# Attention on one core: a planner's order replaced by a written table, with 15 instead of 16 groups of scores on VectorE

## The chip, the cores and the metric

The kernel runs on one core of a Trainium2 chip. The metric is the device time of one execution in microseconds (us). Five engines run side by side, each through its own list of instructions in order, and wait for each other by semaphores: TensorE (PE, with its weight loads as PEld), VectorE (DVE), ScalarE (ACT), GpSimd (POOL) and SyncE (SP), which only issues DMAs here.

## The reference, cut to what matters

Softmax attention over 8 x 8 heads, 512 positions, 64 numbers each, in 32-bit floats:

```python
scores = np.einsum('bhqd,bhkd->bhqk', q, k) / np.sqrt(64)
scores = scores - scores.max(axis=-1, keepdims=True)
attn = np.exp(scores)
attn = attn / attn.sum(axis=-1, keepdims=True)
out = np.einsum('bhqk,bhkd->bhqd', attn, v)
```

## The kernel before, in words

**Tiling.** The 64 heads are worked on as 32 pairs, numbered g = 0 to 31. A head has four blocks of 128 keys. The scores of one block are a tile of 128 keys x 512 queries, and two blocks make a *group*: `[128, 2, 512]` in PSUM, tile `st`, of which there are three buffers. There are 128 groups' worth of scores; the last group is done in two halves (numbers 127 and 128). The maximum is not subtracted.

**The way of one pair.**
- SP loads q, k and v of a pair, 256 KB each (`load`, L509). Each of the three has seven buffers, so a load waits until the buffer of seven pairs earlier has been cast.
- POOL casts each to 16 bits (`cast`: q and k at L525, v at L515). For v a column of ones stands beside the 64 columns, so that the last product also gives the sum of the exponentials.
- PE transposes q and k (`transposes`, L558, four matmuls a call, two calls a pair), and DVE copies the result to SBUF (`copy`, L571).
- PE makes the scores of a group (`scores`, two matmuls at L598 on 64 rows each).
- The exponential of most groups is one ACT instruction over 128x1024 numbers (L602). For some groups DVE makes it in place of ACT: a `raise` (L625) that reads the scores and leaves integer bits in `pd`, and five passes in SBUF (`pass`, number 0 to 4: L642, L651, L659, L661, L665), which leave two factors, `pe` and `pd`. Such a block needs two products where the others need one.
- PE multiplies with v (`values`, L704), one call for 128 queries of one head: four matmuls, and one more for each of its blocks that DVE has made. Seven such units share a PSUM bank `o`.
- For each bank DVE takes the reciprocal of the sums (`rec`, L671) and multiplies (`mul`, L676) into `ring`, which has 112 slots. SP stores from there (`store`, L690 for a pair of heads, L694 for one; the last two go through ACT's queue).
- The last head is done apart (`last`, L720; `finish`, L733 to L740).

**What sets the order.** All instructions are recorded in one order by hand, and each engine keeps its share of it. In the kernel before, the class `Plan` makes this order: it steps through a modelled time with costs for each operation (for instance `EXP` 853 and `EXP_FIXED` 64 ns) and writes down what each engine would do next. The 16 groups in `ON_DVE` go to DVE. `Plan.trigger` chooses behind which VectorE instruction a cast is held: `cast_behind` (L539 and the lines after it) adds a wait of the cast on one of the last six VectorE instructions. Casts before 9000 ns of the planned time have no such wait. For q and k a one-element `memset` on POOL (tile `mark`, L543) waits for the transposes that read the old buffer. In `scores`, the exps of the groups in `KNOWN` also wait for the cast six places back.

The first pair, groups 0 to 2, is written out in `first_pair`; the plan begins with group 3.

Of the kernel before, what the change touches and what calls it, by code (L numbers as in the profile page):

```python
# [17 lines left out]
class Plan:  # L18

    SLOT, EXP, EXP_DONE, EXP_FIXED = 216, 853, 181, 64  # L20
    INTO, OUT_OF = 96, 96
    TRANSPOSE, V_UNIT = 222, 128
    TO_ACT, TO_DVE, TO_PE = 220, 210, 60

    COPY, NORM, RAISE = (601, 690), (50, 133), (1132, 1215)
    RECIPROCAL = 115
    SCALE, PRODUCT, EXTRA = 333, 600, 29
    COPY_1 = (400, 190)
    NORM_COLUMN, PASS_DONE = 67, 115
    PASSES = (SCALE, SCALE, PRODUCT, SCALE, PRODUCT)  # L30
    BITS = 2
    NEEDS = (None, None, 0, 2, 3)
    FIRST_EXP = 5000
    STEP = 5
    CALM, KEEN = 9000, 4
    FIRST_UNIT = 4
    KNOWN, OVER = (13, 15, 18, 20, 22, 24, 27, 42, 50, 61, 69, 97), 6
    ON_DVE = (5, 10, 16, 25, 28, 39, 44, 54, 63, 66, 74, 81, 91, 96, 103, 116)

    LATE_NORM, LATE_COPY, HURRY, SOON, BACKLOG = 700, 1500, 800, 160, 600  # L40
    LATE_MUL, WAIT = 400, 200
    SLACK, AHEAD = 0, 2

    CAST, CAST_PORT, CAST_DONE, TO_POOL = 557, 475, 130, 150
    SCALE_PORT, PRODUCT_PORT, GAP, REACH = 271, 537, 20, 5
    FIRST_LAND, LOAD, STORE, LATENCY, ISSUE = 5200, 752, 376, 2300, 470
    QUEUED, URGENT = 3500, 16
    PAIRED, STORE_ISSUE = 18, 520
    RAW, QK16, NV, NU = 7, 5, 12, 112
    PAIR, DUEK, DUEV, DUEL, PRE = 3300, 3550, 6000, 5000, 0  # L50

    def __init__(self, groups, pairs, first):
        self.groups, self.pairs = groups, pairs
        self.pe, self.act, self.dve = 7000, self.FIRST_EXP, 6300
        self.pool, self.port, self.dma = 4600, 4600, self.FIRST_LAND
        self.m, self.tiled = first, True
        self.read = []
        self.exps = {}
        for m in range(first):
            self.act += self.EXP + self.EXP_FIXED  # L60
            self.exps[m] = self.act + self.EXP_DONE
            self.read.append(self.exps[m])
        self.tq = {0: 5800}
        self.transposed = {0: 5800}
        self.next_t = 1
        self.part_t = 0
        self.banks = [5100, 5800]
        self.todo = [(g, h) for g in range(pairs) for h in range(2)]
        self.last = self.todo.pop()
        self.last_part = 0  # L70
        self.head = None
        self.units = self.FIRST_UNIT
        self.member = {b: m for m, grp in enumerate(groups) for b in grp}
        self.ready = []
        self.passes = []
        self.passed = {}
        self.raised = set()
        self.steps = []
        self.busy_dve = 0
        self.order, self.paired = [], 0  # L80

        late = {grp[0][0] for m, grp in enumerate(groups) if m in self.ON_DVE}
        due = []
        for g in range(pairs):
            scores = 5000 + self.PAIR * g
            if g:
                due += [(scores - self.DUEK, g, "k"), (scores - self.DUEK + 10, g, "q")]
            due.append((scores + self.DUEV + (self.DUEL if g in late else 0), g, "v"))
        self.due = sorted(due)
        self.uncast = list(self.due)  # L90
        self.casts = []
        self.landed, self.cast_done = {}, {}
        self.first_loads = [(g, n) for _, g, n in self.due if g < self.RAW]
        self.first_loads += [(self.RAW, "k"), (self.RAW, "q")]
        for x in self.first_loads:
            self.dma += self.LOAD
            self.landed[x] = self.dma
        self.loads, self.stores, self.stored = [], [], []
        self.sp = 1650 + 470 * len(self.first_loads)

    def note(self, t, *what):
        self.steps.append((t, len(self.steps)) + what)

    def trigger(self, t):

        ops = self.ops
        if not ops or ops[-1][1] <= t - 300:  # L110
            return 1, None
        n = len(ops) - 1
        while (
            n > 0
            and len(ops) - n < self.REACH
            and not ops[n][2]
            and ops[n][0] - ops[n - 1][1] <= self.GAP
        ):
            n -= 1
        if n > 0 and ops[n][0] - ops[n - 1][1] <= self.GAP:  # L120
            n -= 1
        return len(ops) - n, ops[n][1]

    def emit(self, t, back, after):
        _, g, n = self.uncast.pop(0)
        shared = (g, n) == (1, "q")
        self.note(t, "cast", g, n, back if t > self.CALM else 0)
        if not shared:
            self.casts.append((g, n, t if after is None else after + self.TO_POOL))
        if g + self.RAW < self.pairs:  # L130
            self.loads.append((g + self.RAW, n))

    def fits(self, t, soon=0):
        if not self.uncast:
            return False
        _, g, n = self.uncast[0]
        if n != "v" and g >= self.QK16 and self.transposed.get(g - self.QK16, 1e9) > t:
            return False
        return self.landed.get((g, n), 1e9) <= t + soon

    def step_pool(self, t):
        if self.uncast and self.uncast[0][1:] != (1, "q") and not self.casts and self.pool <= t:
            quiet = not self.passes and self.port <= t and not any(x[1] == "raise" for x in self.ready)
            if self.fits(t) and (quiet or self.uncast[0][0] - self.PRE < t):
                self.emit(t, 1, None)
        if self.casts and self.pool <= t and self.port <= t:
            g, n, after = self.casts[0]
            if after <= t and self.landed.get((g, n), 1e9) <= t:
                self.casts.pop(0)
                begin = max(self.pool, self.port, after, self.landed[(g, n)])  # L150
                self.pool = begin + self.CAST
                self.port = begin + self.CAST_PORT
                self.cast_done[(g, n)] = begin + self.CAST + self.CAST_DONE

    def step_sp(self, t):
        if self.sp > t or (self.loads and self.dma > t + self.QUEUED):
            return
        urgent = len(self.stores) > self.URGENT
        if self.loads and not urgent:
            g, n = self.loads[0]  # L160
            if self.cast_done.get((g - self.RAW, n), 1e9) <= t:
                self.loads.pop(0)
                self.note(t, "load", g, n)
                self.dma = max(self.dma, t + self.LATENCY - self.LOAD) + self.LOAD
                self.landed[(g, n)] = self.dma
                self.sp = t + self.ISSUE
                return
        if self.stores and self.stores[0] <= t:
            both = self.both()
            if both and (len(self.stores) < 2 or self.stores[1] > t):  # L170
                return
            heads = 2 if both else 1
            self.note(t, "store", heads)
            self.dma = max(self.dma, t + self.LATENCY - heads * self.STORE) + heads * self.STORE
            for _ in range(heads):
                self.stores.pop(0)
                self.stored.append(self.dma)
            self.paired += heads - 1
            self.sp = t + self.STORE_ISSUE

    def both(self):

        n = len(self.stored)
        g, h, u = self.order[n]
        return (
            self.paired < self.PAIRED
            and g < self.pairs - 2
            and h == 0
            and n + 1 < len(self.order)
            and self.order[n + 1][0] == g  # L190
            and u % self.NU + 8 <= self.NU
        )

    def room(self, t, u):
        heads = (u - self.NU - self.FIRST_UNIT + 3) // 4
        return heads <= 0 or len(self.stored) >= heads and self.stored[heads - 1] <= t

    def free(self, n=0):
        m = self.m + n
        if m >= len(self.groups):  # L200
            return 1e9
        g = self.groups[m][0][0]
        return max(0 if m < 3 else self.read[m - 3], self.tq.get(g, 1e9))

    def for_dve(self, m):
        return m in self.ON_DVE
# [692 lines left out]
```

## Time and profile before

| | |
|---|---|
| time, median of 3 runs | 113.64 us (113.58 to 113.94) |
| the profiled execution | 113.92 us, of which 112.1 us are the span from its first instruction to its last |
| granted TensorE clock | 0.994 of full speed |
| moved by DMA | 33.84 MB, 302 GB/s on average, 336 to 382 GB/s from 11 to 81 us |
| scores on ACT at full width (L602) | 108 of 128x1024, and 2 of half that |
| groups on DVE (L625) | 16 |

The profile page gives the busy time of each engine, a chain of waits that ended last, and groups of instructions by line. An exp that is recorded as started while the one before it still runs looks longer than it is, so several exps can overlap in the sums. Queries of the trace show instructions in order of time, waits by who ended them, and busy time by window. The span of 112.1 us is counted from the first instruction of the program; the profiled execution's own time has 1.8 us more around it.

### The profile page before, as it was taken

What the parts mean: (1) busy time and instruction counts of PE and PEld (TensorE: products, weight loads), DVE (VectorE), ACT (ScalarE), POOL (GpSimd) and SP (SyncE); (2) the same over time, 40 slices, a digit from 0 to 9 for tenths busy, and PEclk for the clock granted to TensorE, in tenths of its full rate; (3) what the DMA queues carried; (4) which work ended last, traced back from release to release, by engine and by line L of the source; (5) the groups of instructions that cost most, each with busy time, mean ns of one, the idle gap of its engine ahead of it and who ended that gap; (6) DMA issues with size and microseconds to landing.
All of it is one profiled execution on the core that took longest, in us unless ns stands there. A gap on an engine that the chain in (4) does not pass through costs nothing.

```text
span 112.1 us, 4408 instructions
## 1 busy us (share of the span) xinstructions
PE 103.2 (92%) x1728; PEld 69.4 (62%) x1728; DVE 100.8 (90%) x227; ACT 105.5 (94%) x118; POOL 65.9 (59%) x127
## 2 busy tenths in 40 slices
PE   7978889999799998999989999899999999999980
PEld 7634555766367766658647767577557577675660
DVE  1647999999999999999999999999999999997390
ACT  4599999999999999999999999999999999999970
POOL 2147768549756886495594786876784855600000
PEclk9999999999999999999999999999999999999997
DMA  3999999999999999999999999999999974142354
GB/s 106 276 359 353 345 350 347 355 336 349 345 347 336 341 346 343 354 364 375 370 358 382 350 355 377 354 372 362 343 366 305 349 245 143 52 141 99 97 167 161
DMA packets 35093, 33.84 MB, mean 302 GB/s; under 512 B 2304, under 2 KB 35072, under 8 KB 35072
## 3 DMA queue, kind: packets, MB, share of 16 engines
q1 hardware_dynamic: 34496, 33.04, 90.4%
q10 hardware_dynamic: 576, 0.52, 1.4%
q8 instruction: 13, 0.21, 0.8%
q14 instruction: 8, 0.07, 0.2%
HBM read 25.17 MB, written 8.39 MB: 299 GB/s over the span
## 4 chain that ended last, share of the span: by engine, by line
DVE 39%; PE 24%; DMA 15%; issue 8%; POOL 7%; SPq 3%; ACT 2%; POOLq 0%; ACTq 0%
PE o L704 13%; DMA v<-in_v_dram 10%; PE st L598 8%; DVE pd L625 8%; DVE tqk L571 7%; DVE ring L676 7%; DMA q<-in_q_dram 5%; DVE m L659 4%; POOL qkp L525 4%; DVE pd L665 4%; POOL vp L515 3%; PE tp L558 2%; SPq L509 2%; DVE m L642 2%; DVE pe L651 2%
## 5 line engine op out<-in xcount | busy, mean ns | idle before, releaser
L602 ACT ACTIVATE pt<-st 128x1024 f16<-128x1024 f32 (+1 forms) x110 | 100.3, 1144 | 0.2 <-PE st L598 0.2
L704 PEld LDWEIGHTS <-pt 128*128 128x128 f16 x880 | 38.8, 98 | 12.1 <-issue 10.2
L704 PE MATMUL o<-vp,pt 128*128 128x65 f16 x880 | 45.3, 194 | 0.4 <-POOL vp L515 0.2
L598 PE MATMUL st<-tqk 64*128 64x512 f16 (+1 forms) x250 | 41.7, 380 | 2.6 <-ACT pt L602 1.4
L525 POOL CAST qkp<-k 128x512 f16<-128x512 f32 x31 | 22.2, 717 | 11.3 <-DVE rc L671 5.3
L525 POOL CAST qkp<-q 128x512 f16<-128x512 f32 x30 | 21.7, 725 | 9.0 <-DVE rc L671 5.3
L515 POOL CAST vp<-v 128x512 f16<-128x512 f32 x32 | 21.4, 679 | 9.2 <-PE st L598 2.4
L676 DVE TENSOR_TENSOR ring<-o,rc 128x448 f32<-128x448 f32 (+2 forms) x37 | 22.3, 606 | 0.4
L704 PE MATMUL o<-vp,pe 128*128 128x65 f16 x128 | 21.8, 194 | 0.0
L704 PE MATMUL o<-vp,pd 128*128 128x65 f16 x128 | 21.7, 192 | 0.0
L558 PE MATMUL tp<-ident,qkp 128*128 128x128 f16 x248 | 19.6, 220 | 1.6 <-DVE tqk L571 0.8
L558 PEld LDWEIGHTS <-qkp 128*128 128x128 f16 x248 | 14.4, 97 | 9.9 <-issue 4.6
L571 DVE COPY tqk<-tp 128x1024 f16<-128x1024 f16 x30 | 20.3, 683 | 0.0
L625 DVE TENSOR_SCALAR pd<-st 128x1024 uint16<-128x1024 f32 x16 | 19.5, 1216 | 0.7 <-PE st L598 0.7
L598 PEld LDWEIGHTS <-tqk 64*128 64x128 f16 x250 | 10.7, 93 | 11.8 <-issue 4.6
L704 PEld LDWEIGHTS <-pe 128*128 128x128 f16 x128 | 12.5, 98 | 3.4 <-issue 3.3
L704 PEld LDWEIGHTS <-pd 128*128 128x128 f16 x128 | 12.5, 98 | 0.0
L659 DVE TENSOR_TENSOR m<-m 128x1024 f16<-128x1024 f16 x16 | 11.0, 685 | 0.0
L665 DVE TENSOR_TENSOR pd<-pd,m 128x1024 f16<-128x1024 f16 x16 | 10.9, 684 | 0.0
L671 DVE RECIPROCAL rc<-o 128x7 f32<-128x7 f32 (+2 forms) x37 | 7.4, 199 | 2.6 <-PE o L704 2.4
L661 DVE TENSOR_SCALAR m<-m 128x1024 f16<-128x1024 f16 x16 | 6.7, 418 | 0.1
L651 DVE TENSOR_SCALAR pe<-pd 128x1024 uint16<-128x1024 uint16 x16 | 6.6, 411 | 0.0
(51 smaller groups left out, 34.9 us busy)
## 6 DMA issues: line engine op xcount, KB each, us to landing
v<-in_v_dram SPq DMA_DIRECT2D x32, 256.0 KB, 5.8
k<-in_k_dram SPq DMA_DIRECT2D x31, 256.0 KB, 5.8
q<-in_q_dram SPq DMA_DIRECT2D x31, 256.0 KB, 5.9
out_dram<-ring SPq DMA_DIRECT2D x18, 256.0 KB, 5.5
out_dram<-ring SPq DMA_DIRECT2D x25, 128.0 KB, 2.2
k<-in_k_dram ACTq DMA_DIRECT2D x2, 128.0 KB, 2.8
q<-in_q_dram SPq DMA_DIRECT2D x2, 128.0 KB, 2.6
out_dram<-ring ACTq DMA_DIRECT2D x2, 128.0 KB, 1.9
```

The source lines that it names most:

```text
L515: return nc.gpsimd.tensor_copy(out=vps[g % NV][:, :, :, 0:D], in_=raw[g]["v"][:, :, :, :])
L525: return nc.gpsimd.tensor_copy(out=dst, in_=src[:, :, :, :])
L558: reads[g] = nc.tensor.transpose(tps[g][:, n, i, :], qkp[g][:, n, i, :], ident)
L571: nc.vector.tensor_copy(out=tqk[g][:, :, :], in_=tps.pop(g).rearrange("p n i c -> p n (i c)"))
L598: nc.tensor.matmul(st[:, x, cols], kc, qc[:, cols], start=True, stop=True)
L602: ins = nc.scalar.activation(out=pt[:, :, cols], in_=st[:, :, cols], func=EXP, scale=scale, bias=SHIFT)
L625: nc.vector.tensor_scalar(out=r["pd"][:, :, :], in0=r["st"][:, :, :], scalar1=BITS, scalar2=BIAS, op0=AluOp.mult, op1=AluOp.add,)
L651: ins = nc.vector.tensor_scalar(out=r["pe"][:, :, :], in0=u[:, :, :], scalar1=0x7C00, scalar2=None, op0=AluOp.bitwise_and,)
L659: ins = nc.vector.tensor_tensor(out=m16, in0=m16, in1=m16, op=AluOp.mult)
L665: ins = nc.vector.tensor_tensor(out=u16, in0=u16, in1=m16, op=AluOp.mult)
L676: nc.vector.tensor_tensor(out=ring[:, u % NU : u % NU + n, :], in0=o[:, x : x + n, 0:D], in1=rcs.pop(u)[:, 0:n].broadcast_to([P, n, D]), o ...
L704: nc.tensor.matmul(os[u // 7][:, u % 7, :], part[:, y * P : (y + 1) * P], vps[g % NV][:, h, c, :], start=(n == 0), stop=(n == len(parts) - 1),
```

## The change

The class `Plan` is gone. A class `Order` holds the order as text instead: one letter for each step (`S` scores, `T` transposes, `V` values of one unit, `C` copy, `R` raise, the letters of `LETTERS` the passes, `N` reciprocal, `M` normalise, `K` cast, `G` load, `w` and `W` stores of one head and of two, `L` and `F` the last head), and beside it the order of heads, casts, loads and banks. A third number in `CASTS` says behind which VectorE instruction a cast is held, counted back from the last one recorded: 2 to 5 for all casts but the first seven, which have none (most often 2). In the order before these numbers run from 1 to 6.

- 15 groups are on DVE where there were 16; the last of them is group 108, where it was 116. The group taken off it is an ACT instruction more, a raise and five passes less, and eight matmuls less at `values`.
- Scores, transposes, values, copies, casts, loads and stores keep their number, apart from that; their places change. Steps of scores that follow each other without other TensorE work between make 91 runs, where they made 74.
- The first 21 loads are the same, but in another order from the 13th on. Of the 73 loads behind them the order changes throughout: the first is pair 9's q, and pair 8's k and q come fifth and sixth.
- `raise_` takes its tiles `pe` and `pd` when it is recorded, where `scores` took them earlier.
- `KNOWN` and the number of buffers of every pool stay as they were; `first_pair` is not changed.

```diff
-class Plan:
...
-    ON_DVE = (5, 10, 16, 25, 28, 39, 44, 54, 63, 66, 74, 81, 91, 96, 103, 116)
...
+class Order:
+
+    ON_DVE = (5, 11, 15, 26, 31, 37, 47, 55, 58, 67, 81, 84, 96, 103, 108)
+    RAW, QK16, NV, NU, FIRST_UNIT, PAIRS = 7, 5, 12, 112, 4, 32
...
+    STEPS = (
+        "SKKTTKCSKSTRKSTSKCVVVKNSGSaMGbTGcTSGKCSGVdGKSRTKVGTSKGCSVVGeSGTgTKGRSVKVVSKNCSKMTTfVkSSh"
...
+    CASTS = (
+        "1k 1q 2k 2q 0v 3k 3q 4k2 4q2 5k3 5q2 1v2 2v4 6k2 6q4 4v2 7k3 7q2 3v2 5v2 8q3 8k3 9k2 9q2 "
...
+    FIRST = "1k 1q 2k 2q 0v 3k 3q 4k 4q 5k 5q 1v 6k 6q 2v 4v 3v 5v 6v 7k 7q"
+    LOADS = (
+        "9q 7v 9k 10q 8k 8q 11q 10k 12q 11k 12k 14k 8v 10v 14q 9v 13k 15q 15k 12v 11v 13q 17k 17q "
...
     def dve(ins):
-        latest[:] = [ins] + latest[: Plan.REACH]
+        trail.append(ins)
         return ins
...
-        if behind and latest:
-            tc.add_manual_dep(ins.ins, latest[behind - 1].ins.name, SYNC, reason="SBUF ports")
+        if behind:
+            tc.add_manual_dep(ins.ins, trail[-behind].ins.name, SYNC, reason="SBUF ports")
...
-            tiles = {n: dpool.tile([P, 2, S], U16, tag=n, name=f"{n}_{m}") for n in ("pe", "pd")}
-            raised[m] = {"st": st, **tiles}
+            raised[m] = {"st": st}
...
     def raise_(m):
         r = raised[m]
+        for n in ("pe", "pd"):
+            r[n] = dpool.tile([P, 2, S], U16, tag=n, name=f"{n}_{m}")
+        for x, b in enumerate(groups[m]):
+            blocks[b] = [r[n].bitcast(FP16)[:, x, :] for n in ("pe", "pd")]
...
-        plan = Plan(groups, NP, 3)
-        steps = plan.run()
+        order = Order()
...
-        for what, *args in steps:
+        for what, *args in order.steps():
             do[what](*args)
```

More of the change, by code (lines that the diff above doesn't have):

```diff
@@ L1 @@
 import math
+import re
 from contextlib import ExitStack
@@ L463 @@
     dpool = ctx.enter_context(tc.tile_pool(name="pd", bufs=4))
-    wpool = ctx.enter_context(tc.tile_pool(name="work", bufs=Plan.BITS))
+    wpool = ctx.enter_context(tc.tile_pool(name="work", bufs=2))
     opool = ctx.enter_context(tc.tile_pool(name="out", bufs=4))
@@ L467 @@
     ps_x = ctx.enter_context(tc.tile_pool(name="ps_x", bufs=1, space=bass.MemoryType.PSUM))
-    NV = 12
-    NU = Plan.NU
+    NV, NU = Order.NV, Order.NU
+    KNOWN, OVER = (13, 15, 18, 20, 22, 24, 27, 42, 50, 61, 69, 97), 6
     ring = cpool.tile([P, NU, D], FP32, name="ring")
@@ L522, in cast @@
         if (g, name) == (1, "q"):
-            nc.vector.tensor_copy(out=dst[:, :, 0:2], in_=src[:, :, 0:2])
+            dve(nc.vector.tensor_copy(out=dst[:, :, 0:2], in_=src[:, :, 0:2]))
             return nc.gpsimd.tensor_copy(out=dst[:, :, 2:4], in_=src[:, :, 2:4])
         return nc.gpsimd.tensor_copy(out=dst, in_=src[:, :, :, :])
-    latest = []
+    trail = []
     reads = {}
@@ L535, in dve @@
     def dve(ins):
-        latest[:] = [ins] + latest[: Plan.REACH]
+        trail.append(ins)
         return ins
     def cast_behind(g, name, behind):
-        if name == "k" and g - Plan.QK16 in reads:
+        if name == "k" and g - Order.QK16 in reads:
             small = nc.gpsimd.memset(mark[0:1, :], 0.0)
-            tc.add_manual_dep(small.ins, reads[g - Plan.QK16].ins.name, SYNC, reason="tile")
+            tc.add_manual_dep(small.ins, reads[g - Order.QK16].ins.name, SYNC, reason="tile")
         ins = cast(g, name)
         behind_it.append(ins)
-        if behind and latest:
-            tc.add_manual_dep(ins.ins, latest[behind - 1].ins.name, SYNC, reason="SBUF ports")
+        if behind:
+            tc.add_manual_dep(ins.ins, trail[-behind].ins.name, SYNC, reason="SBUF ports")
     def transposes(g, n, bank):
@@ L581, in scores @@
         if on_dve:
-            tiles = {n: dpool.tile([P, 2, S], U16, tag=n, name=f"{n}_{m}") for n in ("pe", "pd")}
-            raised[m] = {"st": st, **tiles}
-            parts = [tiles[n].bitcast(FP16) for n in ("pe", "pd")]
+            raised[m] = {"st": st}
         elif half == 1:
@@ L598, in scores @@
             nc.tensor.matmul(st[:, x, cols], kc, qc[:, cols], start=True, stop=True)
-            blocks[(g, c, h)] = [part[:, x, :] for part in parts] if on_dve else [pt[:, x, :]]
+            if not on_dve:
+                blocks[(g, c, h)] = [pt[:, x, :]]
         if on_dve:
@@ L604, in scores @@
         )
-        if m in Plan.KNOWN:
-            tc.add_manual_dep(ins.ins, behind_it[-Plan.OVER].ins.name, SYNC, reason="cast")
+        if m in KNOWN:
+            tc.add_manual_dep(ins.ins, behind_it[-OVER].ins.name, SYNC, reason="cast")
     FIRST, LINEAR, CUBIC = 0.4580331, 1.0167876, 0.1665620
@@ L638, in pass_ @@
             r["m"] = wpool.tile([P, 2, S], U16, tag="m", name=f"m_{m}")
-        u, m16 = r["pd"], r["m"].bitcast(FP16)[:, :, :]
+        u = r["pd"]
         u16 = u.bitcast(FP16)[:, :, :]
+        if s != 1:
+            m16 = r["m"].bitcast(FP16)[:, :, :]
         if s == 0:
@@ L691, in store @@
             return
-        left = 2 * NP - 1 - (u0 + NI - Plan.FIRST_UNIT) // NI
+        left = 2 * NP - 1 - (u0 + NI - Order.FIRST_UNIT) // NI
         queue = nc.scalar if left < 2 else nc.sync
@@ L842 @@
     with tc.manual_schedule():
-        plan = Plan(groups, NP, 3)
-        steps = plan.run()
+        order = Order()
         first_loads()
-        for g, name in plan.first_loads:
+        for g, name, _ in order.read(order.FIRST):
             load(g, name)
```

439 lines of the change are left out of this document (68 added, 371 removed), and 11 rows, old and new, of tables (CASTS, HEADS, LOADS).

## The prediction

> **What bounds the kernel now.** I read the page first. Its busy shares name no winner, and its chain names VectorE (DVE):
>
> ```profile
> PE 103.2 (92%) x1728; PEld 69.4 (62%) x1728; DVE 100.8 (90%) x227; ACT 105.5 (94%) x118; POOL 65.9 (59%) x127
> ...
> DVE 39%; PE 24%; DMA 15%; issue 8%; POOL 7%; SPq 3%; ACT 2%; POOLq 0%; ACTq 0%
> ...
> L602 ACT ACTIVATE pt<-st 128x1024 f16<-128x1024 f32 (+1 forms) x110 | 100.3, 1144 | 0.2 <-PE st L598 0.2
> ```
>
> The chain follows semaphores, and it can lead through any of several engines that are all full. The group row is the better hint: 110 exps on ScalarE (ACT) with 0.2 us of idle time before them in all. The mean of 1144 ns cannot be the rate, since 110 of them would take 125.8 us; neighbours overlap. So I went to the timeline of ACT, one or a few exps at a time (start, length, count):
>
> ```profile
> 7.98 1.06 ACT L602 ACTIVATE pt<-st 128x1024 f16<-128x1024 f32 x1
> 9.21 1.02 ACT L602 ACTIVATE pt<-st 128x1024 f16<-128x1024 f32 x1 [0.18 <-PE st L598]
> 29.33 1.14 ACT L602 ACTIVATE pt<-st 128x1024 f16<-128x1024 f32 x1
> 34.75 2.13 ACT L602 ACTIVATE pt<-st 128x1024 f16<-128x1024 f32 x2
> 59.52 15.89 ACT L602 ACTIVATE pt<-st 128x1024 f16<-128x1024 f32 x17
> 106.49 1.02 ACT L602 ACTIVATE pt<-st 128x1024 f16<-128x1024 f32 x1
> 107.39 1.10 ACT L602 ACTIVATE pt<-st 128x512 f16<-128x512 f32 x2
> ```
>
> Starts mislead here: an exp may be recorded as started while the one before still runs, and then it only looks longer. Ends do not have that fault. The exp that starts at 9.21 is group 4 and ends at 10.23; the one at 106.49 is group 126, the last of full width, and ends at 107.51. Between them stand 107 exps (groups 4 to 126 without the 16 on VectorE), so 106 steps in 97.28 us: **0.918 us a step**. The stretch 29.33 to 36.88 ends seven steps after 30.47: 6.41 / 7 = 0.916. So the slowest stretch and the mean over 97 us agree to 2 ns: from 10.2 us on, ACT never waits. All that it lost lies at the start: group 3 ends at 7.98 + 1.06 = 9.04, group 4 at 10.23, a step of 1.19 where 0.917 would do, 0.27 us lost. The two halves at 107.39 end at 108.49, 0.98 after 107.51, or 0.49 each.
>
> Behind the last exp only a fixed tail follows:
>
> ```profile
> 108.01 0.84 PE L720 MATMUL o_last<-vp,pt 128*128 128x65 f16 x16
> ...
> 108.89 0.18 DVE L733 RECIPROCAL rc_last<-o_last 128x4 f32<-128x4 f32 x1
> 109.10 0.42 DVE L734 TENSOR_TENSOR obl<-o_last,rc_last 128x256 f32<-128x256 f32 x1
> 109.55 0.33 SPq L740 DMA_DIRECT2D out_dram<-obl  x1
> ```
>
> The last product ends 0.36 after the last exp, reciprocal and normalising follow, and the store is issued at 109.55; 112.1 - 108.49 = 3.6 us in all. The span is thus start (to 10.23), 106 steps of ACT, two halves and the tail. **ACT is the bound from 10 us to 108.5 us.**
>
> **The change part by part.** One group of scores goes back from VectorE to ACT (16 to 15). The instruction order of the changed kernel shows 115 activations on ACT where there were 114, the new one at full width. Price on ACT: one step, **+0.917 us**, and nothing hides it, as no gap is left that it could fill after 10.2 us. This is the main term.
>
> [...]
>
> VectorE loses a raise and five passes. What one holds the engine is its step in the chain, where the engine has no gaps (start, length, line: L625 the raise; L642, L651, L659, L661, L665 the passes; L571 a copy; L671 and L676 a reciprocal and a normalising):
>
> ```profile
> 17.36 1.13 DVE pd L625
> 18.49 0.11 DVE rc L671
> 18.61 0.29 DVE pe L651
> 18.90 0.53 DVE ring L676
> 19.43 0.60 DVE m L659
> 20.03 0.34 DVE m L642
> 20.37 0.60 DVE tqk L571
> 20.97 0.11 DVE rc L671
> 21.08 0.29 DVE m L661
> 21.37 0.53 DVE ring L676
> 21.91 0.60 DVE pd L665
> ...
> 87.20 1.15 DVE pd L625
> ```
>
> 1.13 + 0.34 + 0.29 + 0.60 + 0.29 + 0.60 = 3.25 us off VectorE. Was VectorE a second bound that now frees ACT? A window late in the span (its length, then PE, PEld, DVE, ACT, POOL busy) shows it full:
>
> ```profile
> 7.76 0.97 DVE L565 COPY tqk<-tp 128x512 f16<-128x512 f16 x2
> 9.43 1.23 DVE L625 TENSOR_SCALAR pd<-st 128x1024 uint16<-128x1024 f32 x1 [0.70 <-PE st L598]
> ...
> 80.00:90.00 10.00, 9.51 (x140) 5.85 (x140) 9.98 (x21) 10.00 (x12) 7.85 (x15) 1.00 1.04 338
> ```
>
> From the end of the raise of group 5 (9.43 + 1.23 = 10.66) to that of group 103 (87.20 + 1.15 = 88.35) VectorE took 77.69 us; the table's count for it (14 raises, 26 copies, 26 reciprocals and normalisings, 65 passes) makes 75.6 by the rows, so 2.8% more is to be added to such sums. ACT in the same stretch has 84 exps, 84 x 0.917 = 77.03. VectorE fell behind by 0.66 us over 78 us out of its lead, and ACT still took its even steps. A bound that is only almost reached returns nothing when it is relaxed: the 3.25 us are worth **0**. Would the new order make VectorE late? Its tightest stretch is the early one. From the raise of group 5 to that of 37 stand 5 more raises, 9 copies, 7 reciprocals and normalisings and 21 passes, 24.4 x 1.028 = 25.0 us, against 27 exps or 24.8: even. To the raise of 58 it is 41.1 against 45 exps or 41.3, and from 58 to 108 it is 37.4 against 44 exps or 40.3: VectorE gains 3 us there. Worth 0 as well.
>
> TensorE loses 8 products (two blocks, four row blocks each, one term less) and gets another order. Its rows:
>
> ```profile
> 38.35 0.55 PE tp L558 x8
> ...
> 95.54 1.23 PE o L704 x34
> 96.77 0.54 PE st L598 x4
> 97.31 0.36 PE o L704 x8
> 97.67 0.32 PE st L598 x2
> ```
>
> A value product costs (1.23 - 0.36) / 26 = 0.033, a group of scores (0.54 - 0.32) = 0.22, and there is a fixed part of 0.10 ahead of each run of scores and 0.09 behind it. 8 products save 0.27 us; but runs of scores go from 74 to 91 in the table, 17 x 0.19 = 3.3 us more on TensorE. From group 4 to 126: 123 x 0.22 + 88 runs x 0.19 + 60 transposes (4 matmuls each) x 0.225 + 1072 products x 0.033 = 92.7 us, against 107 exps x 0.917 = 98.1. It is hidden beside ACT as a whole; the tight stretch is groups 63 to 98: 36 x 0.22 + 29 x 0.19 + 19 x 0.225 + 364 x 0.033 = 29.7, less group 63's own 0.4, is 29.3 us, against 31 exps or 28.4. TensorE must draw 0.9 us there from a lead that the three score buffers limit: group 63 may be computed once exp 60 has ended, and exps 61 and 62 (1.83) run meanwhile, less 0.32 for the scores themselves and some 0.2 to reach ACT (the first copy ended at 7.76 + 0.97 = 8.73, and group 4's exp began 0.48 later, 0.32 of it scores), or about 1.3. It just fits: cost 0, at worst the 0.2 that a few per cent of hiccups would take beyond it, or 0.7 if the lead at group 63 is but half. I take 0, by the steps that ACT took in the equally full stretches of before.
>
> [...]
>
> Casts (94), loads (73 behind the first 21) and stores (45) keep their number and sizes and only change places. What they cost is a wait:
>
> ```profile
> POOL qkp L525 <- DVE rc L671: 10.7, 16, 1.6
> ...
> PEld L558 <- POOL qkp L525: 3.5, 8, 0.9
> ...
> v<-in_v_dram SPq DMA_DIRECT2D x32, 256.0 KB, 5.8
> ```
>
> Casts are held behind VectorE steps already (first row), and transposes wait for them (second) without ACT noticing. Each wait is queued ahead of all later casts on GpSimd, of a pair's transposes, and through the freed buffer of a load on the in-order SP queue. Loads land 5.8 us after issue; in the new order some loads stand behind a cast by design (pair 14's k waits for the cast of pair 7's). Bounds: 0 when it stays hidden, 0.9 (the longest wait of the second row) once when it does not; below 0 is excluded, as ACT has nothing to give back after 10.2 us. I take 0. The last store but one goes out on the same queues, and the tail's instructions are the same: 0.
>
> **Sum.** 113.92 us of the profiled execution + 0.917 = 114.84. That execution lies 0.28 over the median of the runs, 113.64; on it the forecast is **114.56 us**, 0.8% slower. The bound of what a measurement of this kernel can tell is about 0.3%, 0.34 us.
>
> **Rivals.**
> - **The start gives back its loss.** Group 4 waits for the first copy of pair 1; were that earlier, up to 0.27 us return: 114.29. Against: loads, casts, transposes and copy of pair 1 stand as before. Chance 0.08.
> - **TensorE or a late cast stops ACT.** Place: the tight stretch 63 to 98, or a pair whose cast slips. For: 17 more changes between scores and products, loads in a jumbled order. Price 0.2 to 0.9: 114.8 to 115.5. It decides as soon as the lead at group 63 is under 0.9. Against: groups have more single runs, so a score stands ready earlier. Chance 0.25.
> - **Faster, the exp's step shrinks.** Starts are apart by (34.75 - 29.33) / 6 = 0.903. If the 0.917 came from VectorE's reads of the same score buffers, fewer raises would let it fall; at 0.903 all 107 steps give back 1.5 us: 113.06. It decides from a step of 97.28 / 107 = 0.909 down. Against it stand the windows of the raises' line alone (DVE busy and count):
>
> ```profile
> 29.33:36.00 6.67, 0.00 (x0) 1.00 1.08 341
> 59.52:75.41 15.89, 2.44 (x2) 1.00 1.09 365
> ```
>
> No raise runs in the first, with its step of 0.916; two run in the second, where 17 exps end from 59.52 + 1.2 = 60.7 to 75.41, 16 steps of 0.92. The raise has no hold on the step. Chance 0.03.
> - **The change does nothing** can't be: the new activation is in the built order. A shorter tail together with a better start could bring it within the bound: 0.05.
>
> **How the numbers follow.** Forecast 0.59 (114.4 to 114.75), the cases above 0.08, 0.25, 0.03, 0.05. The range must leave out no more than 0.2: it drops the faster case, the no-change case and the far end of the second rival: 114.2 to 115.3. Faster by over 0.3%: 0.03; within: 0.05; slower: 0.92.
>
> **What would show it.** In the changed profile the ends of the exps step by 0.917 from 10.2 us on, the last ends near 109.4 and the span is near 113.0; VectorE's busy time falls by some 3 us and shows gaps after 60 us; TensorE keeps under ACT. A step of 0.91 or less would prove the faster rival, steps over 0.93 between groups 63 and 98 the second. I am wrong if the last exp ends before 109.1.

## The result, and the profile after

The changed kernel takes 115.08 us (median of 4 runs, 114.91 to 115.29); before takes 113.66 beside it. The ratio is 1.0121, 95% interval 1.0093 to 1.0149: **1.1 to 1.7 us slower**. The forecast was 114.56, so 0.5 us of the loss had not been foreseen. An execution that is over 1.5% longer than the fastest of its kernel counts as slow and stands in no median, ratio or reading here. The profiled execution took 114.91 us, its span is 113.1 us.

The page of the changed kernel, busy time by engine, then the row of the exps (L286 is before's L602). ACT now has no idle time at all before its exps:

```profile
PE 105.6 (93%) x1720; PEld 69.5 (61%) x1720; DVE 99.9 (88%) x221; ACT 106.7 (94%) x119; POOL 63.7 (56%) x127
...
L286 ACT ACTIVATE pt<-st 128x1024 f16<-128x1024 f32 (+1 forms) x111 | 101.5, 1106 | 0.0
```

The timeline of ACT in the changed kernel (start, length, count), at the same kind of places as before:

```profile
8.00 1.98 ACT L286 ACTIVATE pt<-st 128x1024 f16<-128x1024 f32 x2
8.90 1.99 ACT L286 ACTIVATE pt<-st 128x1024 f16<-128x1024 f32 x2
17.93 2.12 ACT L286 ACTIVATE pt<-st 128x1024 f16<-128x1024 f32 x2
20.07 1.02 ACT L286 ACTIVATE pt<-st 128x1024 f16<-128x1024 f32 x1
105.37 1.21 ACT L286 ACTIVATE pt<-st 128x1024 f16<-128x1024 f32 x1
106.60 1.02 ACT L286 ACTIVATE pt<-st 128x1024 f16<-128x1024 f32 x1
107.52 1.51 ACT L286 ACTIVATE pt<-st 128x1024 f16<-128x1024 f32 x2
108.94 0.60 ACT L286 ACTIVATE pt<-st 128x512 f16<-128x512 f32 x1
```

Again read the ends. The pair at 8.90 are groups 4 and 6, and 6 ends at 10.89; the pair at 107.52 are group 126 and the first half of the last group, which ends at 109.03. Between them stand 106 steps of full width and one half, at 0.917 and 0.49 that is 97.69 us; the trace has 98.14. So **0.45 us are late steps**, which the profile of before hardly has (0.07 by the same sum). Two of them can be seen in the rows: the exp at 17.93 and its neighbour end at 20.05, the next at 21.09, a step of 1.04; the one at 105.37 ends at 106.58, the next at 107.62, again 1.04. The idle column misses them (0.0 us in the row of the exps), because an exp that waits shows here as a shorter overlap and not as a gap.

The end of the last exp is 109.54 (108.5 before), and the tail behind it the same 3.6 us. The two profiles differ by 1.03 us of span: one exp 0.92, late steps 0.38 more, less 0.27 that this execution did not lose at its start (group 4 ends at 9.97 instead of 10.24).

What ended the first late step is this piece of the timeline (L200 casts v, L210 q and k, L243 transposes, L281 scores):

```profile
17.34 0.62 POOL L200 CAST vp<-v 128x512 f16<-128x512 f32 x1 [0.44 <-DMA v<-in_v_dram]
...
17.93 0.60 POOL L210 CAST qkp<-k 128x512 f16<-128x512 f32 x1
...
18.48 0.60 POOL L210 CAST qkp<-q 128x512 f16<-128x512 f32 x1
18.59 0.23 PEld L243 LDWEIGHTS <-qkp 128*128 128x128 f16 x4 [0.88 <-POOL qkp L210]
...
19.63 0.60 PE L281 MATMUL st<-tqk 64*128 64x512 f16 x4
```

The cast of pair 2's v waits for its load; the casts of pair 6 stand behind it on POOL; the weight loads of PE wait 0.88 us ahead of the transposes; and the scores come at 19.63, too late for the exp at 20.07. A load is late by 0.44 and ACT loses 0.12.

### The profile page after: what moved, and what is told of

The parts are those of the page before. It is cut to its first block, busy times and chain, and to the rows that moved or that the text cites. A ratio compares the mean times of both kernels' runs of the same rounds, so it can differ in the third digit from the quotient of the medians.

```text
span 113.1 us, 4368 instructions
## 1 busy us (share of the span) xinstructions
PE 105.6 (93%) x1720; PEld 69.5 (61%) x1720; DVE 99.9 (88%) x221; ACT 106.7 (94%) x119; POOL 63.7 (56%) x127
## 4 chain that ended last, share of the span: by engine, by line
PE 41%; DMA 16%; ACT 16%; DVE 15%; issue 5%; SPq 2%; POOL 2%; POOLq 0%
PE o L394 19%; PE st L281 15%; ACT pt L286 13%; PE tp L243 7%; DMA v<-in_v_dram 6%; DMA k<-in_k_dram 5%; DVE ring L366 4%; DVE pd L313 3%; DMA out_dram<-ring 3%; DMA q<-in_q_dram 3%; ACT pt L491 2%; DVE tqk L256 2%; SPq L194 2%; POOL vp L200 1%; DVE pd L355 1%
## 5 line engine op out<-in xcount | busy, mean ns | idle before, releaser
L286 ACT ACTIVATE pt<-st 128x1024 f16<-128x1024 f32 (+1 forms) x111 | 101.5, 1106 | 0.0
L394 PEld LDWEIGHTS <-pt 128*128 128x128 f16 x888 | 39.0, 98 | 17.0 <-issue 14.4
L394 PE MATMUL o<-vp,pt 128*128 128x65 f16 x888 | 48.1, 195 | 0.3 <-DVE ring L366 0.3
L281 PE MATMUL st<-tqk 64*128 64x512 f16 (+1 forms) x250 | 43.7, 382 | 1.0 <-DVE tqk L250 0.5
L200 POOL CAST vp<-v 128x512 f16<-128x512 f32 x32 | 21.8, 687 | 12.6 <-DVE rc L361 5.9
L210 POOL CAST qkp<-k 128x512 f16<-128x512 f32 x31 | 20.9, 676 | 12.9 <-DMA k<-in_k_dram 3.9
L210 POOL CAST qkp<-q 128x512 f16<-128x512 f32 x30 | 20.6, 691 | 9.2 <-DVE rc L361 2.6
L243 PE MATMUL tp<-ident,qkp 128*128 128x128 f16 x248 | 22.0, 220 | 1.7 <-POOL qkp L210 0.7
L243 PEld LDWEIGHTS <-qkp 128*128 128x128 f16 x248 | 14.4, 97 | 10.4 <-POOL qkp L210 4.5
L394 PE MATMUL o<-vp,pe 128*128 128x65 f16 x120 | 20.7, 194 | 0.0
L394 PE MATMUL o<-vp,pd 128*128 128x65 f16 x120 | 20.6, 192 | 0.0
L313 DVE TENSOR_SCALAR pd<-st 128x1024 uint16<-128x1024 f32 x15 | 18.3, 1218 | 0.9 <-PE st L281 0.7
L281 PEld LDWEIGHTS <-tqk 64*128 64x128 f16 x250 | 11.3, 93 | 9.4 <-issue 1.6
L394 PEld LDWEIGHTS <-pe 128*128 128x128 f16 x120 | 11.7, 98 | 1.1 <-issue 0.9
L394 PEld LDWEIGHTS <-pd 128*128 128x128 f16 x120 | 11.8, 98 | 0.0
L355 DVE TENSOR_TENSOR pd<-pd,m 128x1024 f16<-128x1024 f16 x15 | 10.4, 694 | 0.0
L349 DVE TENSOR_TENSOR m<-m 128x1024 f16<-128x1024 f16 x15 | 10.2, 681 | 0.0
L332 DVE TENSOR_SCALAR m<-pd 128x1024 uint16<-128x1024 uint16 x15 | 6.5, 443 | 0.0
```

The lines of the kernel that those rows point to most:

```text
L200: return nc.gpsimd.tensor_copy(out=vps[g % NV][:, :, :, 0:D], in_=raw[g]["v"][:, :, :, :])
L210: return nc.gpsimd.tensor_copy(out=dst, in_=src[:, :, :, :])
L243: reads[g] = nc.tensor.transpose(tps[g][:, n, i, :], qkp[g][:, n, i, :], ident)
L281: nc.tensor.matmul(st[:, x, cols], kc, qc[:, cols], start=True, stop=True)
L286: ins = nc.scalar.activation(out=pt[:, :, cols], in_=st[:, :, cols], func=EXP, scale=scale, bias=SHIFT)
L313: nc.vector.tensor_scalar(out=r["pd"][:, :, :], in0=r["st"][:, :, :], scalar1=BITS, scalar2=BIAS, op0=AluOp.mult, op1=AluOp.add,)
```

## The experiments

The theory: ACT is the bound, the exp costs 0.92, and the other 0.5 come from late steps that begin at casts which just follow their loads. Rivals: VectorE's relief pays something back, TensorE is the cause, or the exp costs all of it. Three sets of four ran, each with before beside it: 113.67 in the first (b15_last to a_tail_s125), 114.00 in the second (after_again to a_16), 113.72 in the third. "Late" is the sum of late steps worked out as above from each kernel's own profile; it counts neither the start (up to group 4) nor lateness of the two halves at the end. It comes from one execution of each kernel; a dash stands where none is read.

| kernel | median, us | ratio to before, 95% interval | late, us |
|---|---|---|---|
| b15_last | 114.69 | 1.0089 (1.0068 to 1.0111) | 0.69 |
| b17_119 | 114.39 | 1.0072 (1.0052 to 1.0091) | 0.33 |
| a_v2_early | 115.75 | 1.0188 (1.0144 to 1.0232) | 0.71 |
| a_tail_s125 | 115.86 | 1.0213 (1.0174 to 1.0252) | 0.67 |
| after_again | 115.36 | 1.0107 (1.0067 to 1.0148) | - |
| a_ld8 | 114.96 | 1.0061 (1.0033 to 1.0089) | 0.27 |
| a_loose | 120.97 | 1.0580 (1.0531 to 1.0629) | 6.55 |
| a_16 | 117.39 | 1.0256 (1.0194 to 1.0319) | 3.76 |
| a_ld8_tail | 115.19 | 1.0129 (1.0100 to 1.0159) | 0.0 |
| b_ld8late | 114.82 | 1.0078 (1.0045 to 1.0112) | 0.59 |
| b_loose | 122.22 | 1.0754 (1.0714 to 1.0795) | 8.64 |
| b_7kq | 113.69 | 0.9983 (0.9962 to 1.0005) | 0.01 |

**b15_last: the one exp by itself.**

```diff
-    ON_DVE = (5, 10, 16, 25, 28, 39, 44, 54, 63, 66, 74, 81, 91, 96, 103, 116)
+    ON_DVE = (5, 10, 16, 25, 28, 39, 44, 54, 63, 66, 74, 81, 91, 96, 103)
```

> The kernel before with one thing changed: group 116, the last that VectorE makes, goes to ScalarE. The order up to there is the same, line for line. Theory (ScalarE is the bound, a group costs it one step): +0.917 us, 114.5 to 114.7 where before has 113.66; the ends of the exps keep their step of 0.917. Rival 1 (VectorE was a second bound, so the 3.25 us it is spared give back what the exp costs): within 0.3 us of before. Rival 2 (the whole loss of the changed kernel, 1.42 us, is this one exp): 115.0 or more.

By the ratio it is 0.77 to 1.26 us over before. The theory's 0.917 lies inside; rival 1 (nothing) and rival 2 (all of the 1.42) lie outside. But its profile also has 0.69 us of late steps, in an order that is before's own up to group 116. The largest comes first, 0.42 at 12 us: pair 0's v lands late, its cast (L515) waits, the products wait for the cast, and the exp for the scores behind them. Before's profile is late by about as much there, for another reason, so that the exp of group 7 ends at 12.06 here and at 12.12 in before. The other four, 0.31 together, stand from 26 to 43 us, where before has none. The first line is the cast at the start; the two others show how the later ones begin (L525 casts q and k, L665 is the last pass):

```profile
9.59 0.62 POOL L515 CAST vp<-v 128x512 f16<-128x512 f32 x1 [0.88 <-DMA v<-in_v_dram]
...
21.66 0.61 POOL L525 CAST qkp<-k 128x512 f16<-128x512 f32 x1 [0.84 <-DMA k<-in_k_dram]
21.77 1.04 DVE L665 TENSOR_TENSOR pd<-pd,m 128x1024 f16<-128x1024 f16 x1
```

The load of pair 7's k lands late, the cast begins late and falls together with a pass, and the pass takes 1.04 us where this line's median is 0.68. The same load is late in the next kernel's profile, b17_119, which keeps before's order up to there, and steps late by 0.12, 0.05, 0.03 and 0.09 follow from 25 to 42 us:

```profile
21.42 1.09 POOL L525 CAST qkp<-k 128x512 f16<-128x512 f32 x1 [1.01 <-DMA k<-in_k_dram]
```

So **the clean profile of before was one execution, not a property of its order.** My forecast had taken it for one.

**b17_119: one group more on VectorE.**

```diff
-    ON_DVE = (5, 10, 16, 25, 28, 39, 44, 54, 63, 66, 74, 81, 91, 96, 103, 116)
+    ON_DVE = (5, 10, 16, 25, 28, 39, 44, 54, 63, 66, 74, 81, 91, 96, 103, 116, 119)
```

> The kernel before with one group more on VectorE: 119, where VectorE had gaps after 100 us. Theory: the last exp ends 0.917 earlier (107.6 instead of 108.5 in the trace) and the time is 112.7, if nothing behind it is late. Rival: values or the passes of 119 become the end of the chain; then the exps still end 0.9 earlier, but a gap of 0.3 to 0.9 appears ahead of the last exps or the last product, and the time is 113.1 to 113.7.

The rival holds, at more than its price: 0.6 to 1.0 us slower than before. The last exp ends at 107.4, earlier as expected, but 5.2 us pass behind it instead of 3.6. In b17_119's timeline of VectorE, the last pass of the new group, its passes' neighbours and the end:

```profile
105.34 0.43 DVE L661 TENSOR_SCALAR m<-m 128x1024 f16<-128x1024 f16 x1
105.69 0.61 DVE L676 TENSOR_TENSOR ring<-o,rc 128x448 f32<-128x448 f32 x1
106.22 0.68 DVE L665 TENSOR_TENSOR pd<-pd,m 128x1024 f16<-128x1024 f16 x1
...
109.49 0.42 DVE L734 TENSOR_TENSOR obl<-o_last,rc_last 128x256 f32<-128x256 f32 x1
```

The pass ends at 106.9, and the products that need it, two reciprocals and two normalisings follow. So 15 groups cost about a microsecond, and a 17th at this place costs 0.8: what ACT gains by it, the passes of the new group give back at the end. Whether a 17th group at an earlier place would pay was not tried.

**a_v2_early and a_tail_s125: two late steps, each at its supposed cause.**

```diff
# a_v2_early
-    FIRST = "1k 1q 2k 2q 0v 3k 3q 4k 4q 5k 5q 1v 6k 6q 2v 4v 3v 5v 6v 7k 7q"
+    FIRST = "1k 1q 2k 2q 0v 3k 3q 4k 4q 5k 5q 1v 2v 6k 6q 4v 3v 5v 6v 7k 7q"
# a_tail_s125
-        "...MwSVwVVVVVVVNVMVSSwVVVVwV..."
+        "...MwSVwVVVVVSVVNVMVSwVVVVwV..."
```

> The changed kernel with the load of pair 2's v two places earlier (13th instead of 15th); nothing else is moved. Theory (the first of the five late steps of ScalarE, 1034 ns at 20 us, comes from this load: its cast is held by it, the casts of pair 6 stand behind it on GpSimd, the transposes and scores behind these): the step at 20 us becomes 0.917, and as TensorE is then 0.5 us further on, the ones at 26, 29 and 33 us (0.24 us in all) shrink too: 0.1 to 0.36 us less than the changed kernel, 114.7 to 115.0. Rival (TensorE is simply full there): the steps only move, and the time stays at 115.0 to 115.1.

> The changed kernel with one step of the table moved: the scores of group 125 stand five units of values earlier, in the middle of a run of ten units (45 products, 1.5 us) that TensorE had ahead of them. Theory (that run makes the late step of 1048 ns at 106.6 us): this step becomes 0.917 and the time 0.13 us less than the changed kernel. Rival (TensorE has been late since before, the run is not it): a late step of 0.05 to 0.13 stays at group 125 or 126, and the time is the same within 0.05.

Both were misses in time. (In the table the scores of group 125 move by four units, not five.) In a_v2_early the steps at 20 and 26 us are gone, as the theory says, but another of 0.53 us too many stands at 30 us. In its timeline, pair 8's cast of q waits for its load, the cast of k follows it, and PE waits for that (its row names the one-element memset that stands behind the cast):

```profile
27.09 0.81 POOL L210 CAST qkp<-q 128x512 f16<-128x512 f32 x1 [0.58 <-DMA q<-in_q_dram]
...
27.89 0.88 POOL L210 CAST qkp<-k 128x512 f16<-128x512 f32 x1
...
28.82 0.45 PEld L243 LDWEIGHTS <-qkp 128*128 128x128 f16 x8 [0.85 <-POOL mark L228]
...
29.87 1.02 ACT L286 ACTIVATE pt<-st 128x1024 f16<-128x1024 f32 x1 [0.43 <-PE st L281]
```

The same mechanism, one load further on. In the table the loads of pair 8 stand fifth and sixth behind pairs 9's and 10's, though its casts come first. In a_tail_s125 the step at 106 us is gone too, but the two halves at the end come 0.78 us late (1.76 us behind group 126 instead of 0.98), and another step is late by 0.36 at 66 us, in the stretch that I had called TensorE's tight one; there the weight loads of PE had waited 0.58 us at 62.9 us for a cast of k, so this too looks like a late cast rather than PE's own work.

**after_again, a_ld8: the loads.**

```diff
# a_ld8, with FIRST as in a_v2_early
-        "9q 7v 9k 10q 8k 8q 11q 10k 12q 11k 12k 14k 8v 10v 14q 9v 13k 15q 15k 12v 11v 13q 17k 17q "
+        "8k 8q 9q 7v 9k 10q 11q 10k 12q 11k 12k 14k 8v 10v 14q 9v 13k 15q 15k 12v 11v 13q 17k 17q "
```

> The changed kernel once more, as a control beside the three others. Theory: one step of ScalarE more (0.917) plus 0.4 to 0.9 us of late steps, at other places than in the first profile where they come from casts that just follow their loads: 114.9 to 115.5, and the late steps cluster from 20 to 35 us and from 63 to 110 us. Rival (the first profile was a lucky one): 115.6 to 115.9, as in the two kernels made from it, a_v2_early and a_tail_s125.

> The changed kernel with loads moved early in the table: pair 2's v 13th as in a_v2_early, and pair 8's k and q ahead of pair 9's q and k, pair 7's v and pair 10's q (first instead of fifth and sixth). Theory (late steps from 20 to 35 us come from casts held by loads that land just then): the waits of the casts for k and q by DMA fall from 3.9 us to under 2.5 us, no late step over 0.1 us is left between 20 and 35 us, and the time is 0.2 to 0.6 us less than after_again. Rival (these late steps come from VectorE or TensorE): they stay, 0.2 to 0.5 us in sum, and the time is the same within 0.15.

after_again has its median inside the theory's range, but its runs spread from 114.64 to 116.15, over the rival's range too: whether the first four runs of the changed kernel (114.91 to 115.29) were lucky stays open.

a_ld8 is the theory's: no late step is left before 88 us, the sum is 0.27, and the time is 0.4 to 1.0 us over before (0.61%), which leaves room for the one exp and little else. Against after_again, run by run, the mean is 0.56 us lower (114.87 against 115.43, 95% interval 0.1 to 1.0). Two loads are moved here, and a_v2_early, which moves one of them alone, gained nothing in time. One part of the expectation failed: the waits of casts for k by DMA fell only to 3.5 us; which load is waited for counts, not the sum.

The converse, in the kernel before:

```diff
# b_ld8late
         steps = plan.run()
+        moved = [(9, "q"), (7, "v"), (9, "k"), (10, "q"), (8, "k"), (8, "q"), (10, "k")]
+        where = [n for n, s in enumerate(steps) if s[0] == "load"][:7]
+        for n, x in zip(where, moved):
+            steps[n] = ("load", *x)
```

> The kernel before with one thing of the change put in: of its first seven later loads (pair 8's k and q first) the order becomes 9q, 7v, 9k, 10q, 8k, 8q, 10k, as in the table. Theory (this order of loads makes the casts of pair 8 wait, and through transposes and copy the scores of group 32): VectorE or GpSimd wait by DMA for k and q some 1 us more, late steps of ScalarE of 0.2 to 0.6 us at 28 to 36 us, and the time is 0.2 to 0.6 us over before. Rival (the casts were the table's fault, not the loads): under 0.1 us over before.

Seven loads in the table's order, with nothing else moved, cost before 0.5 to 1.3 us, more than I had expected. Late steps of its profile, one of its faster executions (114.23 of 114.18 to 115.34), begin at 29.7 us (0.38) and go on to 43 us. They begin where the theory puts them. This is the cast of pair 8's k in before, which waits for nothing, and then the way from the same cast to the late exp in b_ld8late (L558 transposes, L602 exps):

```profile
25.17 0.60 POOL L525 CAST qkp<-k 128x512 f16<-128x512 f32 x1
```

```profile
26.11 0.62 POOL L525 CAST qkp<-k 128x512 f16<-128x512 f32 x1 [1.18 <-DMA k<-in_k_dram]
...
27.85 0.23 PEld L558 LDWEIGHTS <-qkp 128*128 128x128 f16 x4 [0.52 <-POOL qkp L525]
...
28.68 1.94 ACT L602 ACTIVATE pt<-st 128x1024 f16<-128x1024 f32 x2 [0.27 <-PE st L598]
```

So **the order of these loads is shown as a cause**, from both sides.

**a_ld8_tail: the last late step.** It joins a_ld8 and a_tail_s125.

> a_ld8 (pair 2's v and pair 8's k and q loaded earlier) with the scores of group 125 also moved five units of values forward, as in a_tail_s125. Theory (a_ld8 has one late step of 0.13 us at 107 us that stood in all profiles of the table's order, made by the run of ten units): that step is gone or under 0.09, and what is left over before is the one exp: 0.7 to 0.95 us over before. Rival (TensorE is behind as a whole there): a late step of the same size at 108 to 111 us, and the time as a_ld8, 0.95 us over before or more.

The rival holds, and the fix is worse: 1.3% over before. The step at 107 us is gone, but what stands behind it is later. a_ld8's chain at its end first, then a_ld8_tail's (start, length, count of matmuls; L394 is `values`, L281 `scores`):

```profile
104.55 1.50 PE o L394 x44
106.05 0.54 PE st L281 x4
106.59 1.00 PE o L394 x28
107.59 0.32 PE st L281 x2
```

```profile
105.07 0.54 PE st L281 x2
105.61 0.68 PE o L394 x18
106.28 0.54 PE st L281 x2
106.82 1.00 PE o L394 x28
107.82 0.32 PE st L281 x2
```

PE has no gap in either. The moved scores make a run of their own, PE comes to the scores of the last two halves 0.23 us later each, and the last exp ends 0.23 us later (109.84 instead of 109.61), though ACT had been ahead until then. At the end of the table's order PE is a bound beside ACT.

**a_loose, b_loose: what the hold of the casts is worth.**

```diff
# a_loose
-            tc.add_manual_dep(ins.ins, trail[-behind].ins.name, SYNC, reason="SBUF ports")
+            tc.add_manual_dep(ins.ins, trail[-behind - 2].ins.name, SYNC, reason="SBUF ports")
# b_loose (and REACH + 2 instructions kept)
-            tc.add_manual_dep(ins.ins, latest[behind - 1].ins.name, SYNC, reason="SBUF ports")
+            tc.add_manual_dep(ins.ins, latest[min(behind + 1, len(latest) - 1)].ins.name, SYNC, ...)
```

> The changed kernel with each cast held behind a VectorE step two places further back, so it may start some 0.6 to 1.2 us earlier. Theory (holds make casts late, transposes wait for them, and with 29 runs of scores TensorE cannot make that up): TensorE's waits for casts of q and k fall from 4.5 us, late steps of ScalarE fall by 0.1 to 0.4 us, 0.1 to 0.4 less than after_again. Rival (the hold keeps casts off the passes): passes and casts get longer (casts over 0.75 us on average, passes L349 and L355 over 0.72), and the time is the same or up to 0.5 more.

> The kernel before with each cast held behind a VectorE step two places further back, as a_loose. Theory (casts that run beside passes lengthen them, whatever the order; in a_loose the five passes got 0.08 to 0.12 us longer each on average): passes 0.08 to 0.12 longer, 16 x 5 of them, so 6 to 9 us more VectorE work, and as VectorE is full here, the time is 3 to 8 us over before. Rival (only the table's order is so sensitive): under 2 us over before.

In a_loose the theory falls. The rival holds for the passes (L349 0.76 us on average, L355 0.82), not for the casts (all lines under 0.75), and its price was far too low: to let casts start earlier costs 5.6 us in the table's order, against after_again. In before's order it costs 8.5, a little over the theory's range; its five passes are 0.08 to 0.16 us longer on average, 8.6 us in sum. The line of a multiplying pass in the changed kernel, then in a_loose (min, median and max in ns):

```profile
L349 DVE TENSOR_TENSOR m<-m x15: 639/681/703, 12.1 to 100.4; 128x1024 f16<-128x1024 f16 x15
```

```profile
L349 DVE TENSOR_TENSOR m<-m x15: 642/679/1100, 12.9 to 106.9; 128x1024 f16<-128x1024 f16 x15
```

The median stands still and the longest takes 0.4 us more: a pass either is held up and takes up to 1.10 us, or keeps its 0.68. One that is held up in a_loose, with the cast beside it:

```profile
20.30 0.74 POOL L200 CAST vp<-v 128x512 f16<-128x512 f32 x1 [1.06 <-DVE m L332]
20.49 1.09 DVE L349 TENSOR_TENSOR m<-m 128x1024 f16<-128x1024 f16 x1
```

The cast ends at 21.04 and the pass at 21.58, 0.54 later; in b15_last's two lines above it is 22.27 and 22.81, again 0.54. All eight passes of L349 and L355 in a_loose that take over 0.9 us end 0.54 to 0.55 us after a cast that was running when they began or came right behind it; I read that as work which is done once the cast is over. Holding a cast behind a chosen VectorE step is therefore worth several microseconds here, in both kernels (5.6 and 8.5).

**a_16: the exp taken back in the table's order.** `ON_DVE` gets 116, and `STEPS` gets `R` behind the `M` of unit 203, then `a` to `e` behind VectorE steps of groups 108 and units 210 to 224.

```diff
-    ON_DVE = (5, 11, 15, 26, 31, 37, 47, 55, 58, 67, 81, 84, 96, 103, 108)
+    ON_DVE = (5, 11, 15, 26, 31, 37, 47, 55, 58, 67, 81, 84, 96, 103, 108, 116)
```

> The changed kernel with group 116 on VectorE again (a raise and five passes put into the table behind VectorE's steps of that place), 16 groups in all. Theory (0.917 of the loss is the one exp): the last exp ends 0.9 earlier than in after_again and the time is 0.6 to 0.95 us less, 114.0 to 114.5, so that 0.3 to 0.8 us of loss are left, which are the late steps of the new order. Rival (in this order VectorE and TensorE cannot take the group any more at the end, as with 119 in b17_119): exps end 0.9 earlier, the tail behind them grows from 3.6 to over 4.3 us, and the time is within 0.3 of after_again.

Neither text holds. The exps did not end earlier: late steps of 0.35, 0.88, 0.68 and 0.82 us stand from 100 to 111 us, where I had put the passes by hand between others, and one of 0.73 at 21 us. It says that the end of the table's order takes no more VectorE work in that form, and nothing on the price of the exp. The step at 21 us, ahead of the edit, is again a difference between executions.

**b_7kq: a version that might beat both.**

```diff
+        later = [(5, "v"), (4, "v"), (6, "v")]
-        for g, name in plan.first_loads:
+        for g, name in [x for x in plan.first_loads if x not in later] + later:
             load(g, name)
```

> The kernel before with pair 7's k and q loaded ahead of v of pairs 5, 4 and 6 (18th and 19th instead of 20th and 21st or later); its planned order is not touched. Theory (in b15_last, which has before's order up to group 116, casts of pair 7 waited 0.84 and 0.72 us for their loads, began late and ran into passes, one of which took 1.04 instead of 0.69 us; late steps of 0.15, 0.05, 0.03 and 0.08 us followed): no late steps over 0.05 us from 20 to 45 us, 0.1 to 0.3 us less than before in the median: the version that would beat both kernels. Rival (a lucky or unlucky start hides such small things): within 0.1 us of before.

The two loads go 17th and 18th. Its profile is the cleanest of all, 0.01 us of late steps, and its best run (113.36) the fastest of the study. The median is 113.69 against 113.72, and the interval of the ratio reaches from 0.4% faster to 0.05% slower: not told apart from before.

## Why the prediction was right, and where its size was off

- **In the end part luck.** The time lies inside the range (114.2 to 115.3), which had room for the second rival, and not in the case that the forecast bet on (114.4 to 114.75). The last exp's end and the span came near the foretold 109.4 and 113.0 because two misses nearly cancel in that execution, 0.38 us of late steps against 0.27 at the start.
- **ACT is the bound and the exp costs one step: right.** In every profile read here the median distance of two ends is 0.917 or 0.918 us, and in all but b_loose's most exps end 916 to 918 ns apart. b15_last gives 0.77 to 1.26 us for the exp with that kernel's late steps, a_ld8 0.4 to 1.0 with its own.
- **VectorE's 3.25 us are worth 0: right**, by b15_last. That VectorE's busy time would fall by some 3 us was wrong as a sign to look for: 100.8 to 99.9. In b15_last, with before's order, it fell to 98.0, so the new order keeps VectorE busy 1.9 us longer. The gaps that I expected after 60 us are there (9.08 us busy of the 10 from 60 to 70).
- **Casts, loads and stores cost 0: this is the step that failed.** I had bounded it by 0 and 0.9 and taken 0 because, in before's profile, transposes waited for casts "without ACT noticing". That was one execution. The order of seven loads alone costs before 0.5 to 1.3 us, and its repair takes the late steps before 88 us out of the table's order (in both profiles with that repair, a_ld8 and a_ld8_tail). The late steps were 0.45 us in the first profile, which is about what the forecast lacked. I had seen that pair 14's k stands behind a cast "by design" and had not asked which casts stand right behind their load.
- **TensorE costs 0: a little low.** One late step of 0.13 at group 125 stands in the profiles of the changed kernel, a_v2_early, a_ld8 and a_loose and is gone where its scores were moved, so it belongs to PE. In the stretch of groups 63 to 98 the changed kernel's profile has no late step; a_tail_s125 has 0.39 us there and a_16 0.14.
- **Rivals.** The second, "TensorE or a late cast stops ACT", came true beside the forecast, mostly by its loads, at 0.3 to 0.7 us by the late steps, though not in the place named for it (groups 63 to 98) in the first profile. The start gave back 0.27 in that profile, but not by the change: b_7kq and b_ld8late, with before's start, did not lose it either, and four kernels of the table's order lost 0.04 to 0.34 us at group 4 (pair 1's first loads land at other times in each execution: VectorE waited for its q 1.15 us in before's profile, 0.60 in the changed kernel's and 1.20 in a_loose's). The faster rival is out, since the step stayed at 0.917 with 15, 16 and 17 groups.
- **What stays open.** The late steps differ from one execution to the next, so their share in the 1.42 us of the medians is not a fixed number; each kernel has one profile. What the rest of the new order (heads, banks, runs of scores) costs or gains apart from loads and the tail was not tried.

## What to carry to other kernels

Find the bound by the distance between the ends of neighbouring instructions, not by busy shares or the chain: an engine whose ends step evenly has no room, and each instruction put on it costs one whole step (here 0.917 us on ACT; b15_last's one exp came to 0.77 to 1.26 with its late steps). When an order is free of stalls in one profile, ask for the margin of each wait before an edit is priced at nothing; a cast that comes right behind its load can be a stall in the next execution (pair 7's cast of k did not wait for its load in before's profile, and waited 0.84 and 1.01 us for it in those of b15_last and b17_119, with the same order up to there). When loads and their consumers are both written into tables, check the one order against the other.

## What the runs showed of the hardware

A multiplying pass on VectorE that starts while a cast runs on GpSimd can end late: the medians of these passes stay at 0.68 to 0.70 us, single ones take up to 1.12, and those over 0.9 in a_loose end 0.54 to 0.55 us after the cast does. The other way round, it is the cast that is late: in before's profile 14 casts start 0.14 to 0.15 us after such a pass has started, take 1.00 or 1.01 us where the medians of their groups are 0.62 to 0.70, and end 0.47 or 0.48 us after the pass, which keeps its 0.67 to 0.69. One of these pairs (start, length):

```profile
26.92 0.68 DVE L665 TENSOR_TENSOR pd<-pd,m 128x1024 f16<-128x1024 f16 x1
...
27.07 1.01 POOL L525 CAST qkp<-k 128x512 f16<-128x512 f32 x1
```

Two VectorE steps of earlier start for the held casts (87 of 94 in the table) cost 5.6 and 8.5 us in all. The first loads vary by more than I had expected: with the same first twelve loads in the changed kernel's order, VectorE waited for pair 1's q 0.30 us in one profile (a_tail_s125) and 1.20 in another (a_loose), and the step of group 4 was late by nothing in the one and by 0.34 us in the other.
